# Modulation sums by VectorE, and another order of the attention of layer 1, in a three-block kernel on one core

## The chip, the core and the metric

The kernel runs on one core of one Trainium2 chip. The time is that of one execution of the whole program on the device, in microseconds (us), as a median of a few executions. The engines are TensorE (PE, matmuls; PEld is its weight load), VectorE (DVE), ScalarE (ACT), GpSimd (POOL) and SyncE (SP). Here POOL and SP mostly issue transfers.

## The reference, cut to what matters

Two layers and a third block act on 256 tokens of width 1024 (and, in layer 0, on 256 context tokens too). All is fp32. Around each mixer and each feed-forward part stand six modulation vectors per layer, which come from one large product:

```python
s_lat, s_ctx = silu(c), silu(c_ctx)
for l in range(2):
    mod  = s_lat @ ada_w[l] + ada_b[l]         # 1024 -> 6 * 1024: sh1 sc1 g1 sh2 sc2 g2
    modc = s_ctx @ ada_w[l] + ada_b[l]         # layer 1 needs its first two sixths only
    a = rms_norm(h, norm1_g[l]) * (1 + sc1) + sh1
    h = h + g1 * mixer(a, a_ctx)               # even_mixer in layer 0, odd_mixer in layer 1
    h = h + g2 * ffn(rms_norm(h, norm2_g[l]) * (1 + sc2) + sh2)   # swiglu, then 8 experts
```

The odd mixer of layer 1 has two kinds of heads over 256 own and 256 context keys. The window heads (8 query heads, 2 key heads) and the differential heads (4, each with two softmaxes) both normalise and rotate their queries first:

```python
q = apply_rope(rms_norm(q, g), cos, sin)
# window:        s = q @ k * scale, masked to |i - j| <= 128;  p = softmax over [s, sink];  y = p @ v
# differential:  p = softmax(q1 @ k1 * scale) - lam * softmax(q2 @ k2 * scale);  y = p @ v
```

After the two layers a second block follows (a mixer of dilated and low-rank attention, and a feed-forward part).

## The kernel before, in words

The program runs in stages, one behind the other. On the profile's time axis they are: the mixer of layer 0 (0 to 322 us), its swiglu (322 to 680), the odd mixer of layer 1 (norm and transposes 680 to 716, projections 716 to 803, the attention that is left 803 to 873, output projection 873 to 910), the experts (928 to 1351), the mixer of the second block (1364 to 1587) and its feed-forward part (1603 to 1791). Nearly every instruction is recorded at line 47, since all engines are called through `Clock` (lines 25 to 140); the rows are told apart by the names of tiles.

**Weights.** Each fp32 weight block arrives as `raw` (a transfer issued by SP), ACT casts it to `wh`, DVE subtracts and leaves the rest in `wl`, and PE multiplies three times (`mm3`, line 351): high by high, high by low and low by high. A stream `ws` splits two blocks ahead of PE. Where the tokens are on the moving side the activations are called `aT` (`aTh`, `aTl`).

**Who sets the order.** `Clock.note` (line 104) adds an estimated time to each engine as instructions are written, a transfer counting 2 us plus its bytes at a fixed rate. `timed` (line 443) lets the main generator write the matmuls of a stage, and pulls in side tasks (`live`, `pend`) and one background generator (`bg`) when their estimated times are due. `room` (5000 ns) is how far the estimated DVE and ACT may stand ahead of PE for a side task to go on. On the chip each engine then runs its own instructions in exactly the written order.

**The modulation sums.** `ada` (line 645) is the background of the swiglu. It has seven items (one sixth of `ada_w` each): the last gate of layer 0 and all six of layer 1. Of each, eight tiles `araw` of 128 x 1024 are loaded by POOL into four buffers; `ada_sums` (line 637) multiplies each tile in four matmuls with `sZ` (the vector `s` in a column of a 128 x 32 matrix of zeros), half an item (16 matmuls, 32 x 256 out) at a time. The result (`arow`) is added up by DVE or ACT and turned into columns (`mod`) or rows (`gate`).

**Layer 1.** `l1_main` (line 1671) writes five projections with `proj` (line 1405): window queries, context keys and values `ck`, differential keys `dk`, differential queries `qf`, and differential values (into `h`). Behind each, a task is queued: `q_prep` (line 1493) squares, sums (`pss`), takes the reciprocal root (`rstd_of`, line 521, a chain of nine small DVE operations in `nst`), multiplies the queries with it and rotates them (`roped`, line 1424: `xr`, `sw`, and the result in place), and transposes them. `win_task` (line 1536, eight of them, two heads each) makes scores in two banks (`halves`, line 705), adds the mask `gmask` by DVE on 128 of 512 columns, takes the row maximum (`ast`), bounds it by the sink (`nsink`), exponentiates on ACT (`P`), transposes the probabilities on PE (`turned_probs`: `bank<-ident,P`, copied to `PT` by ACT or DVE in turn, `flip`, line 516) and multiplies with the values. `P` and `PT` have three buffers; a window task takes two of each. The differential tasks (`dkt_task`, `diff_task`, lines 1597 and 1608) are queued after the last projection has been written and both `dk` and the queries are prepared. Their transposed keys `dKT` lie in one of four pieces of memory of which the other three go to early loads of expert weights.

Of the kernel before, what the change touches and what calls it, by code (L numbers as in the profile page):

```python
# [24 lines left out]
class Clock:  # L25
# [28 lines left out]
    def uses(cls, ap):  # L54
# [11 lines left out]
        return cls.seen[name]  # L66

# [76 lines left out]
def tile_net(ctx: ExitStack, tc: tile.TileContext, A, out):  # L144
    nc = tc.nc
    Clock.reset()
    PE, ACT, DVE, POOL, SP = (Clock(e, k) for e, k in ((nc.tensor, "PE"), (nc.scalar, "ACT"), (nc.vector, "DVE"),
                                                       (nc.gpsimd, "POOL"), (nc.sync, "SP")))
# [294 lines left out]
    def timed(main, live, pend, bg=None, most=6, room=5000.0, late=2000.0, lead=300.0):  # L443
# [60 lines left out]
    sZ = adap.tile([128, 8, 32], F32, name="sZ", bufs=1)  # L504
    brow = adap.tile([128, 256], F32, name="brow", bufs=1)
# [8 lines left out]
    turn = [0]  # L514

    def flip():
        turn[0] += 1
        return ACT if turn[0] % 2 else DVE


    def rstd_of(ss, w, n, more=None):
# [17 lines left out]
        DVE.scalar_tensor_tensor(y, q, 1.875 * root, y, op0=OP.add, op1=OP.mult)  # L539
        return y  # L540
# [104 lines left out]
    def ada(items, bank, pool, got):  # L645
# [5 lines left out]
        def fetch(i):  # L651
            if i < len(steps):
                l, j, k = steps[i]
                tiles[i] = pool.tile([128, D], F32, name="araw", tag="araw", bufs=4)
                POOL.dma_start(out=tiles[i], in_=A["ada_w"][l][sl(k), sl(j, D)])
# [3 lines left out]
        for v, (l, j, segs) in enumerate(items):  # L659
# [20 lines left out]
            yield DVE.t + 300.0  # L680
            if gate:
                for x in segs:
                    o = notes.tile([4, 256], F32, name="gates", tag="gates", bufs=6)
                    POOL.dma_start(out=o, in_=row[x::32])
                    got["row", l, j, x] = o
                    if l == 0 or j == 2:
                        got[l, j, x] = gates.tile([128, D], F32, name="gate", tag="gate")
                        POOL.dma_start(out=got[l, j, x], in_=spread(o))
            else:
                b = yield from bank.get()  # L690
                for i in range(2):
                    PE.transpose(b[:, sl(i)], row[:, sl(i)], ident)
                yield PE.t + 300.0
                bv = b[:, 0:256].rearrange("p (i g x) -> p x g i", i=2, x=32)
                for x in segs:
                    DVE.tensor_add(mod[:, l, x, j, :].rearrange("p (g i) -> p g i", i=2), bv[:, x],
# [1790 lines left out]
```

## Time and profile before

| what | value |
|---|---|
| median of 3 runs | 1793.44 us (1792.91 to 1794.52) |
| profiled execution | 1793.26 us |
| its span, first to last instruction | 1791.5 us |
| PE busy in the span | 1671.5 us (93%) |
| DVE busy | 1124.4 us (63%) |
| ACT busy | 867.2 us (48%) |
| mean granted TensorE clock | 0.975 |

The profile is of one execution; 1.8 us of its time lie outside the span. A busy share is a mean over stages with different limits, so each stage has to be looked at by itself: the stretches above, with the busy time of each engine in them, are the view to start with. The granted clock is a share of full speed (2.4 GHz), and 0.50 is the lower of two levels (1.2 GHz).

### The profile page before, as it was taken

What the parts mean: (1) busy time and instruction counts of PE and PEld (TensorE: products, weight loads), DVE (VectorE), ACT (ScalarE), POOL (GpSimd) and SP (SyncE); (2) the same over time, 40 slices, a digit from 0 to 9 for tenths busy, and PEclk for the clock granted to TensorE, in tenths of its full rate; (3) what the DMA queues carried; (4) which work ended last, traced back from release to release, by engine and by line L of the source; (5) the groups of instructions that cost most, each with busy time, mean ns of one, the idle gap of its engine ahead of it and who ended that gap; (6) DMA issues with size and microseconds to landing.
All of it is one profiled execution on the core that took longest, in us unless ns stands there. A gap on an engine that the chain in (4) does not pass through costs nothing. (4 is left out here: it accounts for less than half of the span.)

```text
span 1791.5 us, 24425 instructions
## 1 busy us (share of the span) xinstructions
PE 1671.5 (93%) x9594; PEld 1388.5 (78%) x9594; DVE 1124.4 (63%) x1766; ACT 867.2 (48%) x1321; POOL 80.6 (4%) x154
## 2 busy tenths in 40 slices
PE   5999989999999997998879999999997989979998
PEld 5878768777778886875658888788877979769997
DVE  3545556333333357676769899898996566575555
ACT  3333444312222224444447777777764546545443
POOL 1120000131100000000000000000000000000000
PEclk9999999999999999998989999999998999989999
DMA  9862222686632321322319989898965533246552
GB/s 282 285 226 89 95 77 83 215 272 247 234 132 87 102 92 59 118 81 85 106 53 353 349 291 350 301 359 307 358 230 171 164 122 123 90 141 200 188 188 94
DMA packets 187306, 331.33 MB, mean 185 GB/s; under 512 B 8174, under 2 KB 68992, under 8 KB 187184
## 3 DMA queue, kind: packets, MB, share of 16 engines
q1 hardware_dynamic: 172384, 279.73, 46.0%
q0 software_dynamic: 14800, 49.97, 8.2%
q8 instruction: 77, 1.26, 0.3%
q14 instruction: 45, 0.37, 0.1%
HBM read 328.59 MB, written 1.07 MB: 184 GB/s over the span
## 5 line engine op out<-in xcount | busy, mean ns | idle before, releaser
L47 DVE TENSOR_TENSOR wl<-raw,wh 128x1024 fp32r<-128x1024 f32 (+3 forms) x495 | 551.0, 1142 | 230.5 <-ACT wh L47 228.8
L47 ACT CAST wh<-raw 128x1024 fp32r<-128x1024 f32 (+3 forms) x495 | 473.2, 988 | 273.0 <-PE bank L47 263.9
L47 PE MATMUL bank<-aT,wh 128*128 128x512 f32 (+1 forms) x960 | 287.1, 383 | 1.8 <-DVE aT L47 1.6
L47 PEld LDWEIGHTS bank<-aT,wh 128*128 128x128 f32 x960 | 173.9, 188 | 43.6 <-issue 5.0
L47 PE MATMUL bank<-wh,aT 128*128 128x512 f32 (+2 forms) x640 | 185.2, 366 | 2.7 <-DVE aT L47 2.1
L47 PE MATMUL bank<-aT,wl 128*128 128x512 f32 (+1 forms) x480 | 182.1, 379 | 0.0
L47 PEld LDWEIGHTS bank<-wh,aT 128*128 128x128 f32 x640 | 117.6, 190 | 20.4 <-issue 4.8
L47 PE MATMUL bank<-wl,gh 128*128 128x512 f32 (+1 forms) x306 | 114.7, 375 | 2.6 <-DVE wl L47 2.6
L47 PE MATMUL bank<-wl,aT 128*128 128x512 f32 (+2 forms) x320 | 115.5, 361 | 1.6 <-DVE wl L47 1.6
L47 PE MATMUL bank<-wh,gh 128*128 128x512 f32 (+1 forms) x306 | 115.7, 378 | 0.0
L47 PE MATMUL bank<-wh,gl 128*128 128x512 f32 (+1 forms) x306 | 114.8, 375 | 0.0
L47 PEld LDWEIGHTS bank<-aT,wl 128*128 128x128 f32 x480 | 90.1, 188 | 18.9
L47 ACT ACTIVATE P<-bank,ast 128x512 f32<-128x512 f32 (+1 forms) x96 | 56.7, 598 | 91.3 <-DVE ast L47 82.3
L47 PE MATMUL bank<-zT,wh 128*128 128x256 f32 x512 | 90.1, 281 | 0.0
L47 PEld LDWEIGHTS bank<-zT,wh 128*128 128x128 f32 x512 | 79.0, 190 | 0.5
L47 PE MATMUL bank<-wh,xT 128*128 128x384 f32 (+2 forms) x256 | 69.3, 346 | 3.7 <-ACT wh L47 3.1
L47 PE MATMUL bank<-zT,wl 128*128 128x256 f32 x256 | 71.7, 280 | 0.0
L47 PE MATMUL bank<-wh,hidl 128*128 128x512 f32 x176 | 69.2, 393 | 0.9 <-DVE hidl L47 0.9
L47 PE MATMUL bank<-wh,hidh 128*128 128x512 f32 x176 | 69.7, 396 | 0.0
L47 PE MATMUL bank<-wl,hidh 128*128 128x512 f32 x176 | 69.3, 394 | 0.2 <-DVE wl L47 0.2
L47 PEld LDWEIGHTS bank<-wl,aT 128*128 128x128 f32 x320 | 60.8, 190 | 8.8 <-DVE wl L47 2.7
L47 PEld LDWEIGHTS bank<-wl,gh 128*128 128x128 f32 x306 | 57.5, 188 | 12.6 <-DVE wl L47 4.2
(387 smaller groups left out, 3029.3 us busy)
## 6 DMA issues: line engine op xcount, KB each, us to landing
raw<-in_moe_w_dram SPq DMA_DIRECT2D x96, 1024.0 KB, 7.4
araw<-in_ada_w_dram POOLq DMA_DIRECT2D x80, 512.0 KB, 6.3
raw<-in_moe_w_dram SPq DMA_DIRECT2D x48, 768.0 KB, 6.0
raw<-in_w_ff_dram SPq DMA_DIRECT2D x32, 1024.0 KB, 5.5
raw<-in_ffn_w_dram SPq DMA_DIRECT2D x30, 1024.0 KB, 5.3
raw<-in_ev_w_in_dram SPq DMA_DIRECT2D x48, 256.0 KB, 5.5
raw<-in_w_in_dram SPq DMA_DIRECT2D x10, 1024.0 KB, 5.3
raw<-in_w_in_dram SPq DMA_DIRECT2D x12, 768.0 KB, 5.1
```

The costliest lines, as they stand in the source:

```text
L47: r = fn(*args, **kw)
```

## The change

It has four parts.

1. **Modulation sums.** In the swiglu, `ada` gives way to `ada_slow`: DVE multiplies each tile with its scalar and adds it to `acc` (one operation of 128 x 1024 per tile and vector: 10 `tensor_scalar` and 70 `scalar_tensor_tensor`), and PE adds over partitions with a column of ones `oZ` at the end of an item, 40 matmuls in all where 224 were. Two buffers of `araw` and two of `acc` take the place of four `araw`; a load is issued when the tile two before it has been used.
2. **Order.** `room` falls from 5000 to 3500, `flip` picks whichever of ACT and DVE the estimates show earlier rather than one after the other, and many copies out of PSUM ask `flip`. The estimates written during a second pass over the experts that runs only on overflow are taken back.
3. **Window heads.** `P` and `PT` have four buffers, so that two pairs are in flight; PE adds the mask into the score bank (`gmask` against the identity, two matmuls a pair, 16 in all); the query norm is no longer multiplied into the queries but kept in `rq` and given to the exponential as its scale, and multiplied into the row maximum.
4. **Differential heads.** `dKT` lies in two buffers of the gates, all four pieces go to the expert loads at once, and the tasks are queued as soon as the queries are prepared, with a wait for `dk`; each row maximum takes one more small multiplication by `rq`.

```diff
-    def timed(main, live, pend, bg=None, most=6, room=5000.0, late=2000.0, lead=300.0):
+    def timed(main, live, pend, bg=None, most=6, room=3500.0, late=2000.0, lead=300.0):
...
-    def flip():
-        turn[0] += 1
-        return ACT if turn[0] % 2 else DVE
+    def flip(*_):
+        return ACT if ACT.t < DVE.t else DVE
...
+    def ada_slow(items, bank, pool, got):
...
+                tiles[i] = pool.tile([128, D], F32, name="araw", tag="araw", bufs=2)
+                POOL.dma_start(out=tiles[i], in_=A["ada_w"][l][sl(k), sl(j, D)])
...
+            acc = {x: pool.tile([128, D], F32, name="acc", tag="acc", bufs=2) for x in segs}
+            for k in range(8):
+                r = tiles.pop(v * 8 + k)
+                yield max(Clock.ready(r), DVE.t - 3000.0)
+                for x in segs:
+                    if k == 0:
+                        DVE.tensor_scalar(acc[x], r, sT[:, x, k:k + 1], None, op0=OP.mult)
+                    else:
+                        DVE.scalar_tensor_tensor(acc[x], r, sT[:, x, k:k + 1], acc[x], op0=OP.mult, op1=OP.add)
...
+                fetch(v * 8 + k + 2)
...
+            for i, x in enumerate(segs):
+                for g in range(4):
+                    PE.matmul(b[sl(g, 32), 0:256], oZ[:, x, :], acc[x][:, sl(g, 256)], start=(i == 0),
...
-              bg=ada([(0, 5, (0, 1)), (1, 0, (0, 1)), (1, 1, (0, 1)), (1, 2, (0,)), (1, 3, (0,)), (1, 4, (0,)), (1, 5, (0,))],
+              bg=ada_slow([(0, 5, (0, 1)), (1, 0, (0, 1)), (1, 1, (0, 1)), (1, 2, (0,)), (1, 3, (0,)), (1, 4, (0,)), (1, 5, (0,))],
...
-        rP, rP0, rPT = Res(wk, "P", 3), Res(wk, "P0", 3), Res(wk, "PT", 3)
+        rP, rP0, rPT = Res(wk, "P", 4), Res(wk, "P0", 3), Res(wk, "PT", 4)
...
             for t in range(2):
-                roped(heads(x[:, t, :]), 8, r[:, t * 8:t * 8 + 8], gi, t, heads(x[:, t, :]))
-                yield
+                roped(heads(x[:, t, :]), 8, None, gi, t, heads(x[:, t, :]))
+                yield
+            rstd_of(ss, 16, 64, out=rq[gi])
...
-            halves(s, cQT[:, p, sl(t)], cKT[:, kv, :], 512)
+            halves(s, cQT[:, p, sl(t)], cKT[:, kv, :], 512, (sl(1 - t), mask[:, t, :]))
...
-                DVE.tensor_add(s[hh][:, ms], s[hh][:, ms], mask[:, t, :])
                 DVE.reduce_max(out=n1, in_=s[hh], axis=AX, negate=True)
-                DVE.tensor_tensor(out=n1, in0=n1, in1=nsink[:, 2 * p + hh:2 * p + hh + 1], op=OP.min)
-                ACT.activation(out=P[hh], in_=s[hh], func=AF.Exp, bias=n1, accum_out=den[:, hh:hh + 1])
+                DVE.scalar_tensor_tensor(n1, n1, r, nsink[:, 2 * p + hh:2 * p + hh + 1], op0=OP.mult, op1=OP.min)
+                ACT.activation(out=P[hh], in_=s[hh], func=AF.Exp, bias=n1, scale=r, accum_out=den[:, hh:hh + 1])
```

How the built programs differ is shown at three places. In the names, `wh` and `wl` are the split weights, `X`, `hid` and `hidl` the swiglu's own tiles, and an `xN` at the end counts repeats.

**First place, the swiglu.** PE before, around one half item of the sums:

```order
L47 MATMUL bank<-aT,wh 128x256 x2
L47 MATMUL bank<-aT,wl 128x256
L47 MATMUL bank<-araw,sZ 32x256 x16
L47 MATMUL bank<-aT,wh 128x512 x2
L47 MATMUL bank<-aT,wl 128x512
```

PE after, around the matmuls of an item with one vector:

```order
L47 MATMUL bank<-aT,wl 128x512
L47 MATMUL bank<-aT,wh 128x512 x2
L47 MATMUL bank<-aT,wl 128x512
L47 MATMUL bank<-acc,oZ 32x256 x4
L47 MATMUL bank<-aT,wh 128x512 x2
```

The 16 matmuls on `araw` (14 times in the stage) have become 4 on `acc` (or 8, in the three items with two vectors), seven times in the stage. DVE before, in the middle of the swiglu:

```order
L47 TENSOR_TENSOR mod<-bank,vec_85 128x8
L47 TENSOR_TENSOR wl<-raw,wh 128x1024
L47 TENSOR_TENSOR arow<-bank,brow 128x256
L47 TENSOR_TENSOR wl<-raw,wh 128x1024
L47 TENSOR_TENSOR X<-bank,X 128x512 x4
L47 TENSOR_TENSOR wl<-raw,wh 128x1024
L47 TENSOR_TENSOR arow<-bank,arow 128x256
L47 TENSOR_TENSOR wl<-raw,wh 128x1024
L47 TENSOR_TENSOR X<-bank,X 128x512 x4
```

DVE after, at the start of the fourth item:

```order
L47 TENSOR_TENSOR mod<-bank,vec_85 128x8 x2
L47 TENSOR_TENSOR wl<-raw,wh 128x1024
L47 TENSOR_SCALAR acc<-araw,sT 128x1024
L47 SCALAR_TENSOR_TENSOR acc<-araw,sT,acc 128x1024
L47 TENSOR_TENSOR wl<-raw,wh 128x1024
L47 SCALAR_TENSOR_TENSOR acc<-araw,sT,acc 128x1024 x2
L47 TENSOR_TENSOR wl<-raw,wh 128x1024
L47 SCALAR_TENSOR_TENSOR acc<-araw,sT,acc 128x1024
L47 TENSOR_TENSOR wl<-raw,wh 128x1024
L47 TENSOR_TENSOR hid<-bank,hid 128x512 x4
L47 TENSOR_TENSOR hidl<-hid,hidh 128x512 x4
```

Operations on `araw` now stand between the `wl` of the weights and the `hid` and `hidl` on which PE waits.

**Second place, the end of the last projection of layer 1.** DVE before; `COPY h` takes the last values out of PSUM and ends the projection, `PT` are transposed probabilities of a window pair:

```order
L47 TENSOR_TENSOR wl<-raw,wh 128x1024
L47 COPY h<-bank 128x512
L47 TENSOR_TENSOR X<-X,nst 128x512
L47 TENSOR_TENSOR X<-X,gm_2617 128x512
L47 TENSOR_TENSOR xr<-qf,nst 128x512
L47 TENSOR_TENSOR qf<-xr,rt_2621 128x512
L47 TENSOR_TENSOR sw<-xr,rt_2621 128x16x16 x2
L47 TENSOR_TENSOR qf<-qf,sw 128x512
L47 COPY PT<-bank 128x512
L47 TENSOR_TENSOR X<-X,nst 128x512
L47 TENSOR_TENSOR X<-X,gm_2617 128x512
L47 TENSOR_TENSOR xr<-qf,nst 128x512
```

DVE after, while the projection still runs (`wl` are its weights):

```order
L47 TENSOR_TENSOR sw<-qf,rt_2625 128x16x16 x2
L47 TENSOR_TENSOR qf<-qf,rt_2625 128x512
L47 TENSOR_TENSOR qf<-qf,sw 128x512
L47 TENSOR_TENSOR wl<-raw,wh 128x1024
L47 TENSOR_TENSOR X<-X,nst 128x512
L47 TENSOR_TENSOR X<-X,gm_2621 128x512
L47 TENSOR_TENSOR sw<-qf,rt_2625 128x16x16 x2
L47 TENSOR_TENSOR qf<-qf,rt_2625 128x512
L47 TENSOR_TENSOR qf<-qf,sw 128x512
L47 TENSOR_TENSOR wl<-raw,wh 128x1024
L47 TENSOR_TENSOR X<-X,nst 128x512
L47 TENSOR_TENSOR X<-X,gm_2621 128x512
```

The rotation of the differential queries (`xr`, `qf`, `sw`) stood behind the end of the projection and ahead of a `PT`; it now stands ahead of the last two `wl` of the projection, without `xr`. The multiplications on `X` (differential keys of the context) have moved with it.

**Third place, one window pair on DVE** (a pair is two heads). Before:

```order
L47 TENSOR_TENSOR bank<-bank,gmask 128x128
L47 TENSOR_REDUCE ast<-bank 128x1
L47 TENSOR_TENSOR ast<-ast,nsink 128x1
L47 TENSOR_TENSOR bank<-bank,gmask 128x128
L47 TENSOR_REDUCE ast<-bank 128x1
L47 TENSOR_TENSOR ast<-ast,nsink 128x1
L47 TENSOR_TENSOR ast<-ast,sink 128x2
```

After, at the first pair behind the last projection:

```order
L47 SCALAR_TENSOR_TENSOR rq<-nst 128x16
L47 TENSOR_REDUCE ast<-bank 128x1
L47 SCALAR_TENSOR_TENSOR ast<-ast,rq,nsink 128x1
L47 TENSOR_REDUCE ast<-bank 128x1
L47 SCALAR_TENSOR_TENSOR ast<-ast,rq,nsink 128x1
L47 TENSOR_TENSOR ast<-ast,sink 128x2
```

The mask has left DVE, the minimum with `nsink` has become one operation with the multiplication by `rq`, and the first pair's maximum now follows the end of the chain that makes `rq`. On PE the transposes of `dk` for the differential heads stand behind the last matmul of the projection, before and after; three window pairs have their scores ahead of it, before and after.

## Rows read from the trace of the kernel before

**Rows 1.** Busy time of the whole span, from the page: engine, us, share, instructions.

```profile
span 1791.5 us, 24425 instructions
...
PE 1671.5 (93%) x9594; PEld 1388.5 (78%) x9594; DVE 1124.4 (63%) x1766; ACT 867.2 (48%) x1321; POOL 80.6 (4%) x154
```

**Rows 2.** Stretches, and 806.1 to 812.9 alone; the first line names the columns.

```profile
core 0: us, PE busy (x) PEld busy (x) DVE busy (x) ACT busy (x) POOL busy (x), PEclk, DMA share, GB/s
0.00:322.00 322.00, 291.04 (x1986) 240.89 (x1987) 162.13 (x321) 129.19 (x250) 32.77 (x65) 0.97 0.50 158
322.00:680.00 358.00, 356.57 (x1867) 276.69 (x1867) 142.65 (x205) 89.53 (x109) 40.82 (x76) 1.00 0.51 172
716.00:803.00 87.00, 86.46 (x456) 71.35 (x456) 60.02 (x143) 39.39 (x67) 2.11 (x4) 0.97 0.29 97
803.00:872.70 69.70, 55.46 (x398) 41.17 (x397) 53.28 (x133) 32.24 (x82) 0.00 (x0) 0.90 0.22 76
806.10:812.90 6.80, 4.48 (x26) 3.47 (x26) 6.63 (x14) 0.00 (x0) 0.00 (x0) 0.50 1.05 396
```

**Rows 3.** Instructions on tile araw, 320 to 700 us: durations in ns, then transfers.

```profile
L47 PE MATMUL bank<-araw,sZ x448: 379/379/404, 323.1 to 509.1; 128*32 128x256 f32 x150
L47 POOL DMA_DIRECT2D araw<-in_ada_w_dram x52: 527/530/555, 324.0 to 497.0; - x52
...
DMA to landing us min/median/max: 4.0/6.1/9.8
```

**Rows 4.** Timeline of PE around one half item: start, us, engine, operation, count.

```profile
394.93 0.63 PE L47 MATMUL bank<-aT,wh 128*128 128x512 f32 x2
...
395.40 0.40 PE L47 MATMUL bank<-aT,wl 128*128 128x512 f32 x1
...
395.73 1.93 PE L47 MATMUL bank<-araw,sZ 128*32 128x256 f32 x32
...
397.59 0.73 PE L47 MATMUL bank<-aT,wh 128*128 128x512 f32 x2
```

**Rows 5.** DVE groups by shape, 322 to 680: count, busy us, mean ns.

```profile
L47 DVE TENSOR_TENSOR wl<-raw,wh 128x1024 fp32r<-128x1024 f32 x58 | 69.5, 1221 | 85.6 <-ACT wh L47 85.4
```

**Rows 6.** Waits, 322 to 680: engine, line, releaser; total us, times, longest.

```profile
ACT wh L47 <- PE bank L47: 148.6, 34, 6.6
DVE wl L47 <- ACT wh L47: 85.4, 21, 10.6
```

**Rows 7.** Waits of PE, 803 to 872.7, the same columns.

```profile
PE bank L47 <- DVE PT L47: 5.6, 3, 4.1
PE bank L47 <- ACT P L47: 5.6, 8, 2.3
PE bank L47 <- ACT PT L47: 2.6, 4, 1.0
```

**Rows 8.** Timeline behind the last projection of layer 1.

```profile
804.96 0.69 DVE L47 TENSOR_TENSOR xr<-qf,nst 128x512 f32<-128x512 f32 x1
...
807.68 0.68 DVE L47 COPY PT<-bank 128x512 f32<-128x512 f32 x1
...
808.42 1.97 PE L47 MATMUL bank<-PT,ck 128*64 128x128 f32 x14 [4.13 <-DVE PT L47]
```

**Rows 9.** Groups by shape, 700 to 910; the columns of rows 5.

```profile
L47 PE MATMUL bank<-h,PT 128*128 128x128 f32 x64 | 8.9, 285 | 1.8 <-ACT PT L47 1.0 <-DVE PT L47 0.8
...
L47 DVE SCALAR_TENSOR_TENSOR P<-P,ast,P 128x512 f32<-128x512 f32 x8 | 6.0, 752 | 0.4
...
L47 DVE TENSOR_TENSOR bank<-bank,gmask 128x128 f32<-128x128 f32 x16 | 4.7, 292 | 0.0
...
L47 DVE TENSOR_TENSOR xr<-qf,nst 128x512 f32<-128x512 f32 x4 | 2.7, 684 | 0.0
L47 DVE TENSOR_TENSOR ast<-ast,nsink 128x1 f32<-128x1 f32 x16 | 2.6, 159 | 0.5
```

**Rows 10.** Waits of PE in the second block's mixer, 1364 to 1587.

```profile
PE bank L47 <- ACT wh L47: 8.2, 4, 4.2
```

More of the change, by code (lines that the diff above doesn't have):

```diff
@@ L66, in uses, with save, back @@
         return cls.seen[name]
+    @classmethod
+    def save(cls, engines):
+        return [e.t for e in engines], cls.last, {k: [list(u) for u in v] for k, v in cls.seen.items()}
+    @classmethod
+    def back(cls, engines, state):
+        for e, t in zip(engines, state[0]):
+            e.t = t
+        cls.last, cls.seen = state[1:]
     @classmethod
@@ L681, in ada @@
             if gate:
                 for x in segs:
[L683 to L688, printed above, removed]
-            else:
[L690 to L696, printed above, removed]
-                                   ada_b(l, j).rearrange("p (g i) -> p g i", i=2))
-                bank.put()
-                got[l, j] = True
+                    POOL.dma_start(out=brow[x::32], in_=ap_of(A["ada_b"], (l * 6 + j) * D, [[256, 4], [1, 256]]))
@@ new lines, in ada_slow @@
+            yield DVE.t + 300.0
+            row = pool.tile([128, 256], F32, name="arow", tag="arow", bufs=2)
+            b = yield from bank.get()
+            for i, x in enumerate(segs):
+                for g in range(4):
+                    PE.matmul(b[sl(g, 32), 0:256], oZ[:, x, :], acc[x][:, sl(g, 256)], start=(i == 0),
+                              stop=(i == len(segs) - 1), skip_group_check=True)
+            yield PE.t + 300.0
+            if gate:
+                DVE.tensor_add(row, b[:, 0:256], brow)
+            else:
+                ACT.copy(out=row, in_=b[:, 0:256])
@@ L701, in spread, with halves @@
+            bank.put()
+            yield ACT.t + 300.0
+            yield from ada_use(l, j, segs, row, bank, got)
     def spread(o):
         return ap_of(o, 0, [[0, 128], [1, D]])
-    def halves(s, q, k, n):
+    def halves(s, q, k, n, more=None):
         for c in range(0, n, 256):
             for i in range(2):
-                PE.matmul(s[i][:, c:c + 256], q[sl(i, 64)], k[sl(i, 64), c:c + 256], start=True, stop=True)
+                PE.matmul(s[i][:, c:c + 256], q[sl(i, 64)], k[sl(i, 64), c:c + 256], start=(c == 0 or more is None),
+                          stop=True, skip_group_check=more is not None)
+        if more is not None:
+            for i in range(2):
+                PE.matmul(s[i][:, more[0]], ident, more[1], start=False, stop=True, skip_group_check=True)
@@ L872, in loose @@
         def loose():
-            return [adap.tile([128, D], F32, name="araw", tag="araw", bufs=4) for _ in range(4)]
+            return [adap.tile([128, D], F32, name="araw", tag=("araw", "acc")[i % 2], bufs=2) for i in range(4)]
         def pair_of_raws():
@@ L889, in tile_net @@
         POOL.memset(brow, 0.0)
+        POOL.memset(oZ, 0.0)
+        for i in range(2):
+            POOL.memset(oZ[:, i, i:i + 1], 1.0)
         POOL.memset(r2, 0.0)
@@ L949, in pair_unit @@
             for t in range(4):
-                cp(DVE if t == 3 else ACT, qkv[:, t, :], bs[t][:, :384])
+                cp(flip(), qkv[:, t, :], bs[t][:, :384])
             BG.put(4)
@@ L1414, in proj @@
                     dst = yield from dst.get()
-                cp(DVE if i == 3 else ACT, dst[:, i * per:i * per + n, :],
+                cp(flip(), dst[:, i * per:i * per + n, :],
                    b[:, :n * c].rearrange("p (n c) -> p n c", c=c))
@@ L1485, in ck_prep @@
                 yield
-                cp(ACT if kv else DVE, cKT[:, kv, :], b)
+                cp(flip(), cKT[:, kv, :], b)
                 BT.put()
@@ L1989, in tile_net @@
             ws = keep
+            Clock.back(engines, state)
             norm.tiles(0, 2)
```

94 lines of the change are left out of this document (66 added, 28 removed).

## The prediction, made before the changed kernel ran

> **What bounds the kernel now.** I read the busy times of the whole span first: PE is busy for 1671.5 of 1791.5 us [rows 1], so little is idle overall, and what counts is which PE work goes and where PE waits. Next come the stretches [rows 2]. In the swiglu of layer 0 PE is busy 356.57 of 358 us at full granted clock, with DVE at 142.65 us: that stage is PE's, and any matmul that leaves it shortens it, as long as nothing else takes over. In the projections of layer 1 PE has 86.46 of 87 us. Behind them, from 803 to 872.7 us, no engine is full: PE 55.46 and DVE 53.28 of 69.7 us. There the waits decide, so I read the waits of PE in that stretch [rows 7], and the largest of them in the timeline [rows 8]: PE stands for 4.13 us until a `PT` copy on DVE, which started at 807.68 us, behind the rotation of the differential queries (`xr` at 804.96 us and what follows it). Around that wait, from 806.1 to 812.9 us, the granted clock is 0.50 [rows 2], the lower level.
>
> The profiled execution took 1793.26 us, 0.2 us under the median of the runs, and 1.8 us of it lie outside the span. I sum against 1793.3.
>
> **The sums leave PE.** A half item of 16 matmuls shows in the timeline as two rows [rows 4]. The matmuls before it come every 0.235 us (394.93 to 395.40 is two of them), so the next would have started at 395.63; the next matmul on weights starts at 397.59. A half item costs 1.96 us, and there are 14, as the count of records shows (448, two for each matmul, 32 in a half item) [rows 3, 4]: 14 x 1.96 = 27.4 us go. The 40 matmuls with `oZ` have the same shape, at 1.96 / 16 = 0.12 us each: 4.9 us come. Since PE is full there, this is 22.5 us off the end, if DVE can keep up.
>
> **The sums on DVE.** No row of the stage has the new operation. Its nearest row is `wl`, two inputs of 128x1024, at 1.22 us; the same operation at half the size takes 0.75 us where a plain one of that size takes 0.69 [rows 5, 9]. So one lies between 1.22 and twice 0.75, 1.50; I take 1.30, near the first, as only a fixed part seems to differ. Seventy of these and ten multiplications at no more than 1.22 are 91 + 12 = 103 us. DVE then has 246 us of work in a stage of 335, 73%. It has room, but it executes in order, and each sum waits for its `araw`.
>
> That wait is the edit's real price. The built order keeps only two loads in flight: the load for a buffer is issued when the sum on it is done, and between that and the sum on the new tile stand, in the tight runs (first place), one other sum and one or two `wl`, 2.5 to 3.7 us of work [rows 5]. By the PE work written between load and use, at 0.235 us a matmul, 25 of the 56 tiles are used less than 5 us after their load, most of them some 3.9 us after. A load takes 0.53 us to issue and 4.0, 6.1 or 9.8 us to land (least, median, most) [rows 3]. The planner counts 3.6 us. At the median a tight tile is late by 6.6 - 3.9 = 2.7 us, 68 us over all; at the least by 0.6, 15 us. DVE's queue is then 261 to 314 us full out of 335, so it still isn't the bound by sum.
>
> What stands behind a waiting sum is `wl`, `hid` and `hidl`, and behind those PE. The cover is the lead of the splits: ACT waits 148.6 us for PE to give a weight buffer back, and DVE waits for ACT [rows 6], so `wl` is made about as early as its buffers allow, two weight blocks of 24 matmuls or 11 us ahead. A single late tile of 2.7 us vanishes in that, a run of four or five (11 to 14 us less what DVE catches up between) nearly eats it. I take 3 us of PE waits, between 0 and 15. Three last sums now stand in the last part of the stage, ahead of the norm of layer 1, on which PE waits: 1 us (0 to 4, three sums at 1.3). So this part gives -22.5 + 3 + 1 = -18.5 us, between -22.5 and -3.5.
>
> First, on landing: the least in the row is 4.0 us, the median 6.1. The Trainium skill, page "DMA: Bandwidth & Descriptors", section "Latency and other measured facts", says that a lighter load on HBM makes the fixed cost of a transfer smaller. With two `araw` in flight where four were, that would bring landings towards 4.0, the PE waits towards 0 and this part to -21.5; the trace of before doesn't vary the number in flight, so it doesn't decide.
>
> **Layer 1.** Four things move. (a) The rotation of the differential queries goes ahead of the last two `wl` of the projection (second place). The wait of 4.13 us loses its cause, and if PE doesn't stand there, the 6.8 us at half clock [rows 2, 8] would cost 3.4 less: 7.5 in all. What is late next is the first pair's maximum: it now follows a chain of nine small operations of `rq`, about 0.16 us each [rows 9], 1.5 us, so I count -6 (-7.5 to 0). (b) With four `P` and `PT` two pairs overlap. The other PE waits of the stretch are 5.6 + 5.6 + 2.6 - 4.1 = 9.7 us [rows 7]; I let a third go, -3 (0 to -7). (c) The mask on PE: its nearest row is the product of `h` and `PT`, 128x128, 8.9 us for 64 records of 32 matmuls, 0.28 each, and no less than one record, 0.14 [rows 9]. Six of the sixteen lie in the full projection stretch, 1.7 us; ten in the stretch where PE idles 14 of 70 us, where I count half of 2.8. Together +3 (+0.8 to +4.5). (d) DVE loses 4.7 us of masks and 2.7 of `xr` and gains 16 small multiplications by `rq` of 0.16, 2.5 us [rows 9]: 5 us off an engine that is busy for three quarters there, of which I count 1. In the projections DVE has 60 of 87 us, and room for the rotation; PE waits for none of it there. Sum: -6 - 3 + 3 - 1 = -7, between -15 and +3.
>
> The differential heads are not in fact beside the last projection: on PE the transposes of `dk` stand behind its last matmul, as before. I count nothing for that part. The earlier fourth piece for expert weights counts nothing either: the weights of the experts stand behind a norm, not behind a transfer.
>
> **The rest of the order.** `flip` and `room` change who copies what in layer 0 and in the second block's mixer. Sums per engine stay within 5 us. What could move of PE's idle time is at most the 31 us of layer 0, its start among them [rows 2], and 8.2 us on ACT's casts in the second block [rows 10]. I count 0, with 4 us either way.
>
> Sum: 1793.3 - 18.5 - 7 = 1767.8. Of the two uncertain terms the PE waits may well be smaller, so I say 1767.
>
> **The rivals.**
> 1. *DVE's queue takes over in the swiglu; slower.* If `araw` lands like the slowest of before, DVE waits, not PE, set the stage. For: the planner's 3.6 us is under even the fastest landing, and the sums are tightly spaced. Against: the median, and DMA engines that are half idle there (0.51) [rows 2]. It decides once the waits on 25 tiles exceed what DVE has free: to undo the gain of layer 1 too, 246 + 25 x s = 358 + 7 gives s = 4.8 us, a load of 8.7 us from issue to landing. At 9.8 + 0.53 us, s = 6.4, the stage takes 246 + 160 = 406 us, 48 over before: 1834; half way, around 1810. The issue of a load by POOL takes 527 to 555 ns all through the stage, with DVE's two-input `wl` running beside it [rows 3, 5], so nothing there holds a load back. By the Trainium skill, page "SBUF — State Buffer", section "Who interferes with whom", a load issued by GpSimd can starve while VectorE holds the port pair they share, and `tensor_scalar` is named among the operations that can; an operation with two SBUF inputs holds only the read side. By that rule the ten first sums of the items could hold loads back, not the seventy, and the rival would stay under its point; the rows above agree for two inputs and show nothing for the other.
> 2. *Runs of late tiles are only partly covered.* The mechanism of rival 1 in bursts: 10 to 15 us of PE waits in the stage rather than 3. With layer 1 as forecast: 1775 to 1780.
> 3. *Layer 1 doesn't move.* The stretch from 803 us is bound by chains through DVE, ACT and PE in turn; taking away one wait makes the next as long. For: DVE and PE are about equally full. Then the masks cost what the rest brings: 1774 to 1776. This is also what it would be if the change didn't do what it says, as I found for the differential heads.
> 4. *Layer 1 moves more.* Its low clock goes at a second place too and most waits with it: -15, and the swiglu at -21: 1757.
>
> **How the numbers follow.** The forecast (1761 to 1771) has 0.42, rival 2 0.16, rival 3 0.18, rival 4 0.15, rival 1 0.07 (0.05 of it slower than before, 0.02 near it), and 0.02 for something in layer 0 or the second block that takes 10 us or more. The range leaves out rival 1 and half of the ends on either side: 1753 to 1783. Differences under 0.2%, 3.6 us, are about what a measurement of this kernel can tell from no change: faster 0.92, within 0.2% 0.03, slower 0.05.
>
> **What the profile after would show.** The stretch of the swiglu about 18 us shorter with PE still over 97% busy, DVE near 250 us in it, and the sums at about 1.3 us; waits of DVE `acc` on DMA of 15 to 70 us in all. If PE waits on `wl` or `hidl` there by more than 5 us, rival 2 holds; if the stage is over 350 us, rival 1. In layer 1 no PE wait of 4 us on a `PT` behind the last projection and full clock there; the stretch behind it 5 to 8 us shorter. The prediction is wrong if a sum takes over 1.5 us, if landings with two in flight are slower than 6.6 us, or if the time comes from a stage that the change only reorders.

## The result

The changed kernel took 1762.92 us (median of 4 runs, 1759.14 to 1764.03), the kernel before 1793.98 us (4 runs, 1792.91 to 1797.12): a ratio of 0.982, with a 95% interval of 0.980 to 0.984. Forecast were 1767 us, between 1753 and 1783. The profiled execution is the fastest of the four, 1759.14 us with a span of 1757.4.

### The profile page after: what moved, and what is told of

It is laid out like the page before. It is cut to its first block, busy times and chain, and to the rows that moved or that the text cites. A ratio compares the mean times of both kernels' runs of the same rounds, so it can differ in the third digit from the quotient of the medians.

```text
span 1757.4 us, 23849 instructions
## 1 busy us (share of the span) xinstructions
PE 1643.3 (94%) x9258; PEld 1378.9 (78%) x9258; DVE 1205.9 (69%) x1833; ACT 873.6 (50%) x1323; POOL 80.8 (5%) x157
## 5 line engine op out<-in xcount | busy, mean ns | idle before, releaser
L47 DVE SCALAR_TENSOR_TENSOR acc<-araw,sT,acc 128x1024 f32<-128x1024 f32 x70 | 88.1, 1280 | 32.4 <-DMA araw<-in_ada_w_dram 32.3
```

The lines of the kernel that those rows point to most:

```text
L47: r = fn(*args, **kw)
```

## The profile after, by stage

The page's totals of the changed kernel, as [rows 1] for before:

```profile
span 1757.4 us, 23849 instructions
...
PE 1643.3 (94%) x9258; PEld 1378.9 (78%) x9258; DVE 1205.9 (69%) x1833; ACT 873.6 (50%) x1323; POOL 80.8 (5%) x157
```

PE is busy for 28.2 us less, DVE for 81.5 us more. Where the time went is seen by stage. So that a stage can be compared between kernels, it runs here from one mark in the work to the next, and the marks are not the stage bounds of [rows 2]: the *swiglu* from the first matmul on `aT` behind the last transposes of layer 0 to the end of the last product with `hid`; the *projections* to the last matmul on `aT`; the *attention left* to the first matmul on `yw`; the *tail* to the first matmul on `gh`; the *experts* to the last one; *second mixer* to the first matmul on `zT`; *last part* to the end. In us, one profiled execution each; the other kernels are those of the experiments below:

| kernel | layer 0 | swiglu | projections | attention left | tail | experts | second mixer | last part | span |
|---|---|---|---|---|---|---|---|---|---|
| before | 310.0 | 392.4 | 97.8 | 72.5 | 55.4 | 401.0 | 276.5 | 185.9 | 1791.5 |
| after | 305.0 | 370.8 | 98.2 | 59.2 | 55.8 | 403.7 | 276.4 | 188.2 | 1757.4 |
| e1_old_sums | 308.8 | 390.7 | 99.4 | 59.0 | 56.5 | 403.7 | 276.7 | 188.1 | 1783.0 |
| e2_sums_only | 309.7 | 372.4 | 97.1 | 72.9 | 55.2 | 401.1 | 279.2 | 186.1 | 1773.7 |
| e3_mask_dve | 305.1 | 370.7 | 97.7 | 65.6 | 55.2 | 403.9 | 275.0 | 188.5 | 1761.7 |
| e4_three_p | 309.8 | 370.5 | 98.2 | 67.5 | 46.5 | 403.8 | 275.8 | 188.7 | 1760.8 |
| e5_norm_in | 308.2 | 369.9 | 97.0 | 59.3 | 46.8 | 403.9 | 275.1 | 188.6 | 1748.8 |
| e7_norm_in_again | 308.9 | 370.8 | 96.5 | 60.6 | 47.4 | 403.8 | 276.1 | 188.7 | 1752.8 |
| e6_old_order | 305.1 | 373.3 | 103.8 | 59.6 | 47.7 | 403.7 | 278.3 | 189.4 | 1760.8 |
| e10_tail | 309.2 | 370.1 | 97.5 | 60.1 | 47.3 | 403.7 | 276.5 | 188.8 | 1753.2 |
| e11_no_rq | 308.0 | 372.4 | 97.1 | 59.3 | 47.1 | 400.9 | 276.4 | 184.6 | 1745.7 |
| e12_one_load | 308.1 | 368.7 | 125.3 | 59.1 | 54.0 | 404.0 | 275.0 | 188.6 | 1782.8 |
| e13_before_tail | 304.4 | 391.5 | 97.8 | 72.5 | 47.2 | 400.8 | 277.0 | 185.1 | 1776.3 |
| e14_few_sums | 308.7 | 367.6 | 99.0 | 59.2 | 55.9 | 403.7 | 276.2 | 188.9 | 1759.3 |

Of the profiled 34.1 us, 21.6 lie in the swiglu and 13.3 in the attention that is left behind the projections. The experts and the last part, which the change doesn't touch, got 5.0 us longer. The 5.0 us of layer 0 are mostly this execution's: e4_three_p has the same instructions there and took 309.8.

These are the stretches of the changed kernel, with the columns of [rows 2]: length, busy time (count) of PE, PEld, DVE, ACT and POOL, granted clock, DMA share, GB/s.

```profile
305.00:675.80 370.80, 366.13 (x1689) 294.73 (x1690) 252.56 (x320) 106.86 (x141) 42.12 (x78) 1.00 0.52 171
676.60:774.00 97.40, 90.20 (x467) 74.29 (x466) 71.93 (x165) 45.34 (x76) 2.11 (x4) 0.96 0.33 109
774.00:833.20 59.20, 50.35 (x438) 40.72 (x437) 48.27 (x133) 32.49 (x75) 0.00 (x0) 0.97 0.23 85
833.20:889.00 55.80, 41.21 (x182) 31.78 (x182) 34.63 (x84) 21.32 (x35) 0.55 (x1) 0.82 0.24 80
```

The swiglu is PE's as before, 366 of 371 us busy, with DVE now at 253 us. The attention that is left has a granted clock of 0.97, where it was 0.90 [rows 2]. Before, two stretches of 6.8 us in it lay at the lower level, the one of [rows 2] and a later one; both are gone, and one of 3.4 us has come at another place. First the later one of before, then the one after:

```profile
836.80:843.60 6.80, 6.80 (x32) 4.54 (x34) 4.50 (x11) 3.78 (x12) 0.00 (x0) 0.50 0.00 0
```

```profile
826.60:830.00 3.40, 3.40 (x17) 3.15 (x16) 2.57 (x10) 1.12 (x3) 0.00 (x0) 0.51 0.00 0
```

Next, the instructions that write `acc`, then POOL's loads of `araw`: durations in ns (min, median, max), first and last start; last, landings in us. They answer to [rows 3].

```profile
L47 PE MATMUL bank<-acc,oZ x80: 379/379/403, 365.5 to 665.1; 128*32 128x256 f32 x80
L47 DVE SCALAR_TENSOR_TENSOR acc<-araw,sT,acc x70: 1275/1280/1287, 324.5 to 660.7; 128x1024 f32<-128x1024 f32 x70
L47 DVE TENSOR_SCALAR acc<-araw,sT x10: 745/748/753, 323.2 to 620.2; 128x1024 f32<-128x1024 f32 x10
```

```profile
L47 POOL DMA_DIRECT2D araw<-in_ada_w_dram x54: 530/530/555, 324.9 to 652.8; - x54
...
DMA to landing us min/median/max: 3.8/4.5/8.1
```

One sum takes 1.28 us (1.30 was taken), a first product 0.75. Loads land in 4.5 us, where they took 6.1 with four in flight [rows 3]. While the loads ran, the core moved 183 GB/s here (325 to 655 us) and 247 before (324 to 500). The Trainium skill, page "DMA: Bandwidth & Descriptors", section "Latency and other measured facts", has the fixed cost of a transfer fall with a lighter load on HBM; the trace agrees in direction, but doesn't show the fixed part of a landing by itself. Issuing a load still takes 530 ns, and 555 at most. No issue of a load overlaps a first product, and only five overlap a sum, so the case doesn't test the port that the Trainium skill, page "SBUF — State Buffer", section "Who interferes with whom", has VectorE and GpSimd share.

What PE waits for in the swiglu, and then in the attention left (us in total, times, longest), the latter answering to [rows 7]:

```profile
PE bank L47 <- DVE wl L47: 2.9, 2, 1.6
PE bank L47 <- DVE aT L47: 1.5, 3, 0.9
PE bank L47 <- DVE hidl L47: 0.9, 1, 0.9
```

```profile
PE bank L47 <- DVE PT L47: 6.0, 3, 2.7
PE bank L47 <- DVE dKT L47: 1.7, 1, 1.7
PE bank L47 <- ACT P L47: 1.1, 3, 0.7
```

In the attention left the waits of PE fell from 14.5 to 8.8 us, and no wait of 4 us stands behind the projection any more. DVE's own waits for `araw` add up to 37.7 us in 18 times, inside the 15 to 70 that were forecast.

One wait the change left as it was. From the tail of the changed kernel, PE and ACT around it (a row: start, length, engine, operation, count, idle time before and what ended it):

```profile
844.65 0.39 PE L47 MATMUL bank<-wh,yw 128*128 128x512 f32 x1
...
844.88 0.60 PE L47 MATMUL bank<-ident,PT 128*128 128x128 f32 x4
...
855.95 0.67 ACT L47 ACTIVATE sl<-bank,slg 128x512 f32<-128x512 f32 x1
856.65 0.62 ACT L47 CAST yd<-sl 128x512 fp32r<-128x512 f32 x1
```

```profile
857.32 0.80 PE L47 MATMUL bank<-wh,yd 128*128 128x512 f32 x1 [6.23 <-ACT yd L47]
```

The four transposes of the last differential output (`ident,PT`) stand behind all 48 matmuls on `yw`; their copy `sl` stands on ACT behind the norm of the first half of the output, so PE has run out of work for 6.23 us when `yd` comes. The granted clock is 0.59 in the 4.2 us after it. The kernel before has the same wait, 6.2 us. The experiments showed that it goes with a small change of order.

## The experiments

**Apart: the sums alone, and all but the sums.** e1_old_sums calls the old generator, e2_sums_only puts the new one into the kernel before.

```diff
 # e1_old_sums, from the changed kernel
-              bg=ada_slow([(0, 5, (0, 1)), (1, 0, (0, 1)), ...
+              bg=ada([(0, 5, (0, 1)), (1, 0, (0, 1)), ...
 # e2_sums_only, from the kernel before: ada_slow, oZ and the two tags of araw and acc added, and
-              bg=ada([(0, 5, (0, 1)), (1, 0, (0, 1)), ...
+              bg=ada_slow([(0, 5, (0, 1)), (1, 0, (0, 1)), ...
```

> The changed kernel with the sums on PE again (the background generator of before, two buffers of each of two tags), everything else as changed. If the parts add: the swiglu, from the first matmul on its activations to its last product with hid, goes back from 370.8 us to 392 (as before), the start of the swiglu stays near 305 and the stretch from the last projection of layer 1 to its output product near 59: about 1784 us (1780 to 1788), which leaves 10 us for the order of layer 0 and layer 1. Rival: the gain of layer 1 comes from the sums too (DVE reaches layer 1 in another state); then that stretch goes back towards 72 and the time to 1790 or more.

> The kernel before with the sums on DVE alone. If the parts add: layer 0 and the stretch behind the last projection as before (start of the swiglu at 310 us, 72.5 us), the swiglu about 371 us instead of 392: 1772 us (1769 to 1776). Rival: in the profile after, PE's matmuls in the swiglu came every 0.229 us, before every 0.233; if that is chance between executions and not part of the change, 5 to 6 of the 21.6 us are no gain and the time is about 1777.

Measured: e1_old_sums 1785.62 us, 0.997 of before (0.996 to 0.998); e2_sums_only 1774.28 us, 0.990 (0.987 to 0.992). The parts are apart. In the profiles the sums are worth 20.0 us of the swiglu added to the kernel before (392.4 to 372.4) and 19.9 taken from the changed one (390.7 to 370.8), and the attention left is 59.0 us without them and 72.9 with them alone. The swiglu of the kernel before, then of e2_sums_only:

```profile
310.00:702.40 392.40, 389.97 (x2057) 305.27 (x2058) 165.23 (x245) 106.48 (x139) 40.82 (x76) 1.00 0.47 159
```

```profile
309.70:682.10 372.40, 367.62 (x1689) 294.21 (x1690) 252.57 (x320) 106.86 (x140) 41.96 (x78) 1.00 0.53 170
```

PE is busy 22.4 us less there and DVE 87.3 us more. The rival of e2_sums_only holds by a little: PE's pace in the swiglu is no part of the sums (below), but over the whole stage the matmuls of 512 columns come every 0.2321 us before, 0.2320 in e2_sums_only and 0.2308 after, and this is 1.6 us of the stage, not 5 to 6. Together the two are 23.4 us in medians, not 31. In the profiles the sum falls short by 7.8 us, of which 3.5 lie in layer 0 and 3.0 in the second mixer. In both, profiles with the same instructions differ by about as much: layer 0 took 310.0 us in before and 304.4 in e13_before_tail, the second mixer 276.5 in before and 279.2 in e2_sums_only.

**What the attention gained from.** Three parts were undone one at a time.

```diff
 # e4_three_p
-        rP, rP0, rPT = Res(wk, "P", 4), Res(wk, "P0", 3), Res(wk, "PT", 4)
+        rP, rP0, rPT = Res(wk, "P", 3), Res(wk, "P0", 3), Res(wk, "PT", 3)
 # e3_mask_dve
-            halves(s, cQT[:, p, sl(t)], cKT[:, kv, :], 512, (sl(1 - t), mask[:, t, :]))
+            halves(s, cQT[:, p, sl(t)], cKT[:, kv, :], 512)
...
+                DVE.tensor_add(s[hh][:, sl(1 - t)], s[hh][:, sl(1 - t)], mask[:, t, :])
 # e5_norm_in (and the same in the differential heads)
-                roped(heads(x[:, t, :]), 8, None, gi, t, heads(x[:, t, :]))
+                roped(heads(x[:, t, :]), 8, r[:, t * 8:t * 8 + 8], gi, t, heads(x[:, t, :]))
...
-                DVE.scalar_tensor_tensor(n1, n1, r, nsink[:, 2 * p + hh:2 * p + hh + 1], op0=OP.mult, op1=OP.min)
+                DVE.tensor_tensor(out=n1, in0=n1, in1=nsink[:, 2 * p + hh:2 * p + hh + 1], op=OP.min)
...
```

> The changed kernel with three buffers of P and of PT as before. If two pairs in flight carry part of the gain of layer 1: the stretch from the last projection to the output product goes from 59.2 us to 62 to 66, and PE waits on P or PT there grow by as much. Rival: the gain is the moved rotation and the shorter work of DVE, and the buffers give nothing: 58 to 60.5 us.

> The changed kernel with the mask added by DVE again (16 additions of 0.29 us), not by PE. If DVE is what the stretch from the last projection to the output product is short of: ten of them lie there, 2.9 us, and the stretch goes from 59.2 us to 61 to 63; the output product to the experts stays at 55.8. Rival: PE is as short, its ten mask matmuls cost what DVE gains, and the stretch stays at 58 to 60.

> The changed kernel with the query norms multiplied into the queries again (xr back, no scale in the exponential, no multiplications of the maxima). If the rotation of the differential queries is what kept DVE behind the last projection: it falls back behind the projection, the PE wait of some 4 us on PT and the low clock there return, and the stretch goes from 59.2 us to 66 to 72. Rival: the planner finds room for it ahead of the end of the projection all the same; then 59 to 62.

Measured, one execution each: 1762.63, 1763.51 and 1750.57 us. In kernels that have the same instructions there, the attention left differs by up to 1.3 us (59.0 to 60.1, 59.3 to 60.6, 72.5 to 72.9 in the table). With three buffers the attention left takes 67.5 us, 8.3 more, and PE's waits there are again those on `P`:

```profile
PE bank L47 <- ACT P L47: 3.3, 4, 2.1
PE bank L47 <- DVE PT L47: 3.3, 3, 2.4
PE bank L47 <- ACT PT L47: 2.7, 5, 1.1
PE bank L47 <- DVE P L47: 2.1, 3, 1.4
```

The order has moved along: the four multiplications on `X` and most of a chain to `rq` now stand behind the projection. So the 8.3 us are the buffers' together with what the planner made of them.

With the mask on DVE it takes 65.6 us, 6.4 more, which is over the 61 to 63 that were expected. The stretch of e3_mask_dve, in the columns above:

```profile
773.40:839.00 65.60, 51.38 (x405) 41.20 (x404) 56.91 (x157) 32.54 (x75) 0.00 (x0) 0.92 0.22 81
```

DVE has 8.6 us more in it than after (56.91 against 48.27), PE 1.0 more, and the clock is 0.92, with 10.2 us at the lower level instead of 3.4. The additions themselves are only 2.9 us of DVE's 8.6. The rest is mainly work that the planner moved behind the projection: half of the rotation of the differential queries (2.2 us), the multiplications on `X` (2.8) and most of a chain to `rq` (1.2). From DVE and PE at that place, where `COPY h` ends the projection:

```profile
773.47 0.69 DVE L47 COPY h<-bank 128x512 f32<-128x512 f32 x1 [1.26 <-PE bank L47]
...
776.92 0.69 DVE L47 TENSOR_TENSOR qf<-qf,sw 128x512 f32<-128x512 f32 x1
```

```profile
777.67 0.55 PE L47 MATMUL bank<-ident,qf 128*128 128x128 f32 x3 [1.01 <-DVE qf L47]
```

So e3_mask_dve undoes the mask and half of the rotation's move at once, and its 6.4 us can't be shared out between the two. With the norm back in the queries nothing is lost: 59.3 us. The rival of e5_norm_in held: its rotation is all but done with the projection, the last `qf` ending at 776.0 us and the projection at 775.1. So no run shows what the rotation's place is worth alone.

What e4_three_p and e5_norm_in gave unasked is the tail: 46.5 and 46.8 us where it was 55.8. In both built orders the last transposes stand ahead of the last 12 matmuls on `yw`.

**The rules of order, and the tail.** e6_old_order puts back `room`, `flip` in turn and the fixed engines of the copies. e7_norm_in_again is e5_norm_in once more, in several rounds. e10_tail changes nothing but the place of the transposes and of the `sl` and `yd` made from them, by letting the planner pull side tasks in earlier from the first matmul on `yw` on:

```diff
 # e6_old_order
-    def timed(main, live, pend, bg=None, most=6, room=3500.0, late=2000.0, lead=300.0):
+    def timed(main, live, pend, bg=None, most=6, room=5000.0, late=2000.0, lead=300.0):
...
-    def flip(*_):
-        return ACT if ACT.t < DVE.t else DVE
+    def flip():
+        turn[0] += 1
+        return ACT if turn[0] % 2 else DVE
 # e10_tail (timed takes lead as a list)
             bs = yield from BG.several(4)
+            early_[0] = 1500.0
             for c in range(2):
                 yield from gemm(4, (yw[:, 0], yw[:, 1]), ...
...
-        timed(main, live, pend, most=8)
+        timed(main, live, pend, most=8, lead=early_)
```

> The changed kernel with the old rules of order: room 5000, flip in turn, and the copies on the engines of before; sums, masks, norms and buffers as changed. If the rules of order are what moved the rotation and shortened the stretch behind the last projection: that stretch goes from 59.2 us to 66 to 72, with a PE wait of 3 us or more on PT near its start. Rival: the buffers and the shorter DVE work do it alone; then 58 to 62. In its built order the last transposes of the differential heads stand ahead of the last 12 matmuls on yw, as in the two runs whose tail (output product to the experts) took 46.5 and 46.8 us, and not behind all 48 as in the changed kernel (55.8 us): its tail should take 46 to 48 us too. Layer 0 near 310 us in either case.

> The same kernel as e5_norm_in, for an interval: the changed kernel with the query norms multiplied into the queries. If its 1750.6 us hold: 1748 to 1755 us, 0.976 to 0.979 of before, and 8 to 12 us under the changed kernel, all of it in the tail (46.8 against 55.8 us) where no wait on yd stands. Rival: one lucky execution; then 1757 to 1763.

> The changed kernel with one difference in its order: the four transposes of the last differential output stand ahead of the last 18 of the 48 matmuls on yw, not behind them (the lead of the planner is 1500 ns from there on). If the place of these transposes is the whole tail: PE's 6.2 us wait on yd goes, the low clock behind it too, a wait of up to 2 us on PT comes instead, the tail takes 46 to 50 us instead of 55.8 and the time is 1753 to 1758. Rival: the tail of e5_norm_in is short for another reason (its shorter chain of differential heads); then the wait moves to PT in full, and the tail stays over 53 us.

Measured: e6_old_order 1762.61 us (one execution), e7_norm_in_again 1752.53 us (1750.34 to 1754.62; 0.978 of before, 0.976 to 0.979), e10_tail 1754.70 us (1753.15 to 1756.18; 0.979, 0.978 to 0.981). e10_tail has PE's waits in the tail without the one on `yd`:

```profile
PE bank L47 <- DVE X L47: 4.1, 1, 4.1
PE bank L47 <- DVE sel L47: 2.7, 1, 2.7
PE bank L47 <- DVE P L47: 1.3, 1, 1.3
PE bank L47 <- DVE lgT L47: 0.5, 1, 0.5
```

The tail takes 47.3 us, 8.5 less: 6.2 of wait, and the rest is PE's time, 38.7 us busy where it was 41.2, with 10.2 us at the lower level instead of 20.5. So the place of four transposes is the whole difference, and the norm has no part in it.

By the marks the old rules of order lose nothing in the attention left (59.6, the rival), but they had four window pairs' scores ahead of the mark instead of three. The projections take 5.6 us more, and projections and attention left together 163.4 instead of 157.4. The swiglu takes 2.5 more, with 3.4 us at the lower level where the changed kernel has none. The good tail hides all that in the time. Layer 0 shows no gain from the new rules: with the old ones it took 305.1 us.

**The same in the kernel before.** e13_before_tail has the edit of e10_tail, with a lead of 2500, in the kernel before.

> The kernel before with one difference in its order: the transposes of the last differential output stand ahead of the last 12 of the 48 matmuls on yw instead of behind all (a lead of 2500 ns in the planner from there on). If the place of these transposes is the whole wait on yd: the tail from output product to experts goes from 55.4 us to 46 to 48 and the time to 1782 to 1787. Rival: before has no work to cover with there, the wait moves, and the time stays over 1789.

Measured: 1781.68 us (1778.10 to 1782.31), 0.994 of before (0.992 to 0.996). The tail takes 47.2 us instead of 55.4. This edit is independent of the change.

**Memory.** The experts and the last part took 401 and 186 us in the kernels without the tiles `rq` and about 403.8 and 188.5 in all that have them, with the same instructions. e11_no_rq is e5_norm_in without these tiles, which it doesn't use:

```diff
-        rq = [sm.tile([128, 16], F32, name="rq", tag="rq", bufs=2) for _ in range(2)]
```

> The kernel of e5_norm_in without the two small tiles rq, which nothing uses there: the same instructions in the same order, with every tile that is allocated behind them 128 bytes per partition lower, where the kernel before has them. In all profiles so far the experts took 401 us and the last feed-forward part 186 where these tiles are not, and 403.8 and 188.5 where they are, with matmuls of the same shape every 0.2299 and 0.2331 us; in the swiglu it was the other way round (0.2333 and 0.2294). If the place in memory sets that pace: the experts 401, the last part 186, the matmuls of the swiglu back to 0.233, and 1747 to 1752 us. Rival: the pace comes from something else that the two families of kernels differ in; then every stage as in e5_norm_in, and 1750 to 1755.

Measured: 1747.81 us (1747.43 to 1748.97), 0.975 of before (0.973 to 0.978), against 1752.53 for e7_norm_in_again. The instructions and their order are the same; only the tiles allocated behind `rq` lie 128 bytes per partition lower. First e5_norm_in, then e11_no_rq, experts and last part:

```profile
881.20:1285.10 403.90, 395.24 (x1871) 328.14 (x1868) 364.20 (x401) 308.07 (x377) 0.00 (x0) 1.00 0.92 323
1560.20:1748.70 188.50, 180.78 (x1154) 163.00 (x1152) 104.91 (x113) 84.17 (x99) 0.53 (x1) 0.99 0.49 165
```

```profile
883.90:1284.80 400.90, 391.89 (x1870) 327.71 (x1868) 363.73 (x401) 307.36 (x377) 0.00 (x0) 1.00 0.93 325
1561.20:1745.70 184.50, 176.77 (x1154) 160.19 (x1152) 104.85 (x113) 84.24 (x99) 0.53 (x1) 0.99 0.49 169
```

PE is busy 3.4 and 4.0 us less with the same matmuls at the same granted clock, and the other engines are busy for the same time. Kernels run beside it show the same split: 404.0 and 403.7 us of experts with the tiles (e12_one_load, e14_few_sums), 400.8 without (e13_before_tail). In the swiglu it is the other way: 372.4 us in e11_no_rq against 369.9. This is the fastest kernel of the study.

**The swiglu's queue.** e12_one_load fetches the next tile only after the one before it has been used; e14_few_sums leaves out 60 of the 70 additions and keeps all loads.

```diff
 # e12_one_load
         fetch(0)
-        fetch(1)
...
-                fetch(v * 8 + k + 2)
+                fetch(v * 8 + k + 1)
 # e14_few_sums
-                    else:
+                    elif k == 7:
                         DVE.scalar_tensor_tensor(acc[x], r, sT[:, x, k:k + 1], acc[x], op0=OP.mult, op1=OP.add)
```

> The changed kernel with one load of araw in flight instead of two. Now each of the 56 sums waits for nearly a whole load, 0.53 us of issue and some 4.5 of landing, less the 3.6 that the planner allows for: DVE has 235 us of work, and 56 loads in a row with their sums are 56 x 5.0 + 96 = 376 us. If DVE's queue decides from the point where its work and waits fill the stage (rival 1 of the prediction), the swiglu goes from 371 to 385 us or more and PE waits on wl and hidl by 15 us or more. Rival: the lead of the splits covers single late tiles whatever their number, and the stage stays under 377.

> The changed kernel with 60 of the 70 additions of the sums left out (of each item only the first and the last tile is added), all loads still made. If the sums on DVE are what PE waits for in the swiglu (5.3 us of waits in the profile after): the stage goes from 370.8 to 365 to 368 us. Rival: those waits are the stage's own; it stays at 370 to 371.

Measured, one execution each: 1784.62 and 1761.06 us. e14_few_sums has a swiglu of 367.6 us, so the sums on DVE cost the stage 3.2 us, 2.8 of them in PE waits: those on `wl` are gone, and 2.5 us of waits on `aT` and `hidl` stay, which before has too. e12_one_load went another way than either expectation: its swiglu is even shorter, 368.7 us, and PE waits on `wl` no more than after (1.6 us). Its loads land in 4.4 us, hardly earlier than with two in flight. But the planner, which counts a time for each load, doesn't get the sums done in the stage, and writes the rest behind it, alone. The stretch behind the last product with `hid`, and PE's longest wait in it:

```profile
676.90:711.30 34.40, 0.92 (x8) 0.23 (x8) 19.33 (x32) 5.76 (x11) 3.16 (x6) 0.55 0.47 148
```

```profile
PE bank L47 <- DVE acc L47: 33.6, 1, 33.6
```

PE stands for 33.6 us, where after it stands 7.2 for the norm of layer 1. The price of a slow chain of loads is real, as rival 1 had it, but it appears as sums left over at the end, not as late weights.

## Why the prediction was right

**The swiglu**, forecast at -18.5 us, is 21.6 shorter. At PE's pace of before it is 20.0 (e2_sums_only), and the terms hold: PE is busy 22.4 us less, where 22.5 were counted, and the sums cost 3.2 us (e14_few_sums), where 3 were taken. The 1 us for the sums at the end was nothing: PE's wait for the norm of layer 1, behind the stage, is 7.2 us after and was 8.15 before. DVE got 87.3 us of work there, where 103 were counted; the landings came out at 4.5 us, nearer the lower end, and half of the 68 us of waits with them. Rivals 1 and 2 didn't occur: DVE's work and waits are 290 of 371 us, and PE's waits on `wl` and `hidl` are 3.8 us.

**Layer 1**, forecast at -7, is 12.5 shorter from the end of the swiglu to the experts. Here the sign came out, but not the terms.

(a) The rotation, -6. The wait of 4.13 us and the half clock around it are gone, as forecast, but full clock doesn't hold all through: 3.4 us at the lower level have come at 826.6 us. The 1.5 us for a late chain to `rq` were nothing: `rq` is done at 774.8 us, and DVE then waits 2.8 us for PE's scores. What the rotation is worth by itself stays open.

(b) The four buffers, -3. This term was the most under-sized: 8.3 us come back without them, order included.

(c, d) The mask on PE and the shorter DVE work, +3 and -1. Putting the mask back on DVE costs 6.4 us, so moving it was no loss; but half of the rotation went back with it, and the mask's own share isn't shown. The terms had priced PE's mask matmuls by their busy time and DVE's 5 us as 1, on the ground that DVE was busy for three quarters.

The two runs make up 14.7 us of a stretch that gained 13.3, so their shares overlap and can't be added. Some of the 13.3 us is the clock's: 10.2 us fewer lie at the lower level. By the two profiles of the kernel of e5_norm_in, which have none and 5.1 us there and differ by 1.3 us, that would be about 2.6 us; it is 5.1 at most, if PE takes twice as long at half clock. Both are estimates. The differential heads did not move beside the projection, as said, and the norm in the exponential is worth nothing: 59.3 us without it.

**The rest**, forecast at 0 with 4 us either way, is the sum of things that I hadn't seen: the experts and the last part 5.0 us longer through 128 bytes of memory, and layer 0 shorter by an amount that most executions don't repeat. So the time came out 4 us under the forecast because layer 1 gave 5.5 us more, the swiglu 3 us more, and memory took some back. That it lies so near is in part luck: the misses in layer 1 and in memory, neither of them foreseen, had opposite signs.

Rival 4, the one beyond the forecast, was half right in its mechanism: the low clock went at a second place in layer 1 too, but a shorter one came at a third, and PE's waits only fell from 14.5 to 8.8 us.

## What to carry to other kernels

Where one engine is full, work that another can take is worth its full time, less the waits that its new queue puts in; count those from the distance between load and use, and see whether they fit the lead of what stands behind. Where no engine is full, neither waits nor busy shares gave the right prices here: the added buffers, priced at 3 us, were worth some 8. Where a planner writes the order, undoing one part moves others too, so look in the trace at what else has moved before its price is put down to that part. A planner's order should be read at the last step of a stage: four transposes put 12 to 18 matmuls earlier were worth 8.5 us here.

## What the runs showed of the hardware

**Pace.** Back-to-back matmuls come at two paces with the granted clock at 1.00, and where tiles lie in SBUF has a part in which. In the last part, matmuls of 256 columns; first e5_norm_in, then e11_no_rq:

```profile
1579.73 0.28 PE L47 MATMUL bank<-zT,wl 128*128 128x256 f32 x1
...
1580.79 0.28 PE L47 MATMUL bank<-zT,wl 128*128 128x256 f32 x1
```

```profile
1580.78 0.39 PE L47 MATMUL bank<-zT,wh 128*128 128x256 f32 x2
...
1581.80 0.28 PE L47 MATMUL bank<-zT,wh 128*128 128x256 f32 x1
```

From the first row to the second of each it is nine matmuls: 1.06 us or 0.118 each, and 1.02 us or 0.113 each. In e5_norm_in nearly the whole last part goes at the slower pace; in e11_no_rq it changes to and fro in long runs. For 512 columns in the experts the mean distance of neighbouring starts is 0.2332 and 0.2303 us. In the swiglu it is the other way round, 0.2306 and 0.2321, and both paces, 0.229 and 0.233, take turns in either kernel; the expectations above took 0.229 and 0.233 for the whole stage. That a shift of all later tiles by 128 bytes does this is shown; which operand it is, and why one stage gains where another loses, is open.

**The clock after equal waits.** In layer 0 the changed kernel and e4_three_p run the same instructions. In both PE waits 2.40 us on `P`, and 32 records of the same matmuls follow; first after, then e4_three_p:

```profile
117.43 1.93 PE L47 MATMUL bank<-araw,sZ 128*32 128x256 f32 x32 [2.40 <-ACT P L47]
```

```profile
119.45 3.56 PE L47 MATMUL bank<-araw,sZ 128*32 128x256 f32 x32 [2.40 <-ACT P L47]
```

They take 1.93 us in one and 3.56 in the other. The same wait is followed by a fall of the clock in one execution and not in another; in e5_norm_in and e12_one_load the fall came some 9 us later. Layer 0 takes 304 to 305 us in the four profiles that have no stretch at the lower level between 110 and 140 us, and 308 to 310 in the ten that have one. A difference of 4 us in one profile is not yet the kernel's.
